# Scale steps of the float16 input projection: fixed places on VectorE, a unit more between them on TensorE, and the transpositions of queries and keys a unit later

## The chip, the cores and the metric

One NeuronCore of a Trainium2 chip runs the whole kernel. The metric is the device time of one execution in microseconds (us). Before the change it was 2442.49 us, the median of 3 runs (2439.93 to 2445.21). Five engines work side by side, each through its own instructions in order: TensorE (PE, matmuls and transpositions into PSUM), VectorE (DVE), ScalarE (ACT), GpSimd (POOL) and SyncE (SP, which here only issues DMAs). They wait for each other through semaphores.

## The reference

One layer of a hybrid decoder, on a sequence of 2048 rows with 1024 columns. Only the first half of it bears on the change:

```python
sh1, sc1, g1, sh2, sc2, g2 = jnp.split((c_act @ w_ada + b_ada)[:, None, :], N_MOD, axis=-1)
h = rmsnorm(x, norm1_g) * (1 + sc1) + sh1
proj = h @ w_in                       # 1024 x 3080
q, k, v, fg, xin, bg, cg = jnp.split(proj, IN_SPLITS, axis=-1)
q = rmsnorm(q.reshape(b, s, ATTN_HEADS, HEAD_DIM), q_norm_g)
k = rmsnorm(k.reshape(b, s, ATTN_HEADS, HEAD_DIM), k_norm_g)
attn = forgetting_attention(q, k, v, log_sigmoid(fg + b_forget))
conv = bg * causal_dwconv(cg * xin, conv_mix_w)
x = x + g1 * (jnp.concatenate([attn, conv], axis=-1) @ w_out)
# then a gated feed-forward network with a causal convolution (w_up, w_down)
```

## The kernel before, in words

**Numbers in two halves.** The projection runs in float16, and every operand is held as a high and a low half: hi = float16(scale x raw) and lo = scale x raw - hi. `scaled_split` makes them, the high half on ScalarE (L195), the low one on VectorE (L196). A product takes three matmuls (`mm3`, L142): hi hi, hi lo, lo hi. The scale is a power of two that comes from the data: `weight_group` sums the magnitudes of each raw weight tile on ScalarE (`weigh`, L191), takes the largest on VectorE (L215), and `power_of_two` brings it to all partitions in two steps. Its first step is a transposition on TensorE (L170), with a maximum and a small product on VectorE (L172, L173); its second a matmul with ones on TensorE (L176), and five tiny VectorE instructions (L177 to L181). Only then can the splits begin.

**Stages on TensorE.** From 0 to 54 us the modulation of the first normalization is computed, interleaved with the first of four chunks of h. Up to about 163 us the values are projected, 16 units of 128 rows: `transpose_in` turns a chunk of x, one column block k at a time (L348), ScalarE evacuates it with scale and shift (L350), GpSimd and VectorE make the two halves (L136, L353; chunk 0 in other forms first, L355 and L356). Chunk 0 of the values still uses unscaled weights; later ones use `wv16`, split by `first_scales`. ScalarE evacuates each value unit (L454, L455). Then come the key units (16, to 257.7 us), the query units (16, to 359.7), four conv groups of 64 us each (twelve units each, products for x, c and b of four chunks), and from about 627 us attention, the output projection and the feed-forward network.

**Key and query units (`project`).** A unit is 24 matmuls of 128x512. Behind it ScalarE squares the result (sq, L632), VectorE sums and takes the reciprocal root (r, rqt; L634 and L123 to L129) and scales (qn, L638). `finish` transposes qn on TensorE (L606), in the middle of a later unit: of the unit two behind. ScalarE evacuates the transposition (tf, L612), GpSimd and VectorE split it (th, tl; L136, L614) and SP stores the halves (L616). In between, hooks of single units do other work: `piece`, part of the later modulation, sums rows of `w_ada` that SP loads (L660) on VectorE into mo (L662, L664), and a piece later multiplies the sum on TensorE (L669 or L684); others make the cumulative sum of the forget gates (L525) and the largest value (L562).

**What sets the order.** Instructions given to K (`keep_in_program_order`) keep their place on their engine in program order; matmuls and transpositions all do. The others are placed by the scheduler. `weight_group` and `first_scales` are generators: each `next(group)` at the end of a unit carries out the part up to the next yield, so a yield is a distance of one unit. The magnitudes of `w_up` for the feed-forward network are also taken during these stages: `magnitudes` reduces one 128x512 tile on ScalarE (wx, L708) and has SP load the next into the only wx buffer (L713); both are pinned, twice in each of the units of a `lull` (key units 0 to 12, query units 2 to 14) and once behind each conv unit.

**Buffers.** PSUM tiles with the tag "tr" (transpositions, scale steps, L525, L562, the modulation products) share the two buffers of ps_t; unit results have six in ps_m. Raw weights (wr), high (wh) and low (wl) pairs have eight each, vt, qn and wm two, wx one.

## Time and profile before

| what | us |
|---|---|
| median of 3 runs | 2442.49 |
| the profiled execution | 2440.35 |
| its span on the core | 2438.5 |
| TensorE busy | 2336.2 (96%) |
| VectorE busy | 1802.1 (74%) |
| ScalarE busy | 1307.1 (54%) |
| GpSimd busy | 338.6 (14%) |

A row of a timeline gives the start and the duration in us, the engine, the line, the operation and its tiles (out<-in), and in brackets how long the engine was idle just before and which instruction of which engine ended the wait. A row of a window gives its length and the busy time and count of each engine in it, the granted clock of TensorE (1.00 is full), the busy share of the DMA engines and GB/s.

### The profile page before, as it was taken

To read this page: it belongs to the slowest core of one execution; us is meant where nothing else is said; L and a number is where in the kernel's file an instruction comes from. 1 tells how busy PE (TensorE), PEld (TensorE's weight loads), DVE (VectorE), ACT (ScalarE), POOL (GpSimd) and SP (SyncE) were. 2 spreads that over 40 slices of the span, in tenths; PEclk is the share of its full clock that TensorE was granted. 3 is DMA by queue.
4 is the path that set the end of the run, shared out by engine and by line. 5 is a ranking of instruction groups with operands and counts; after the bars stand their busy time and mean duration, and the time that the engine had idled before them with its cause. 6 is when DMAs were issued, how large, how long until landed. Compare 5 with 4: busy or idle time off the path is not lost.

```text
span 2438.5 us, 38643 instructions
## 1 busy us (share of the span) xinstructions
PE 2336.2 (96%) x14472; PEld 1405.9 (58%) x14472; DVE 1802.1 (74%) x3430; ACT 1307.1 (54%) x2136; POOL 338.6 (14%) x282
## 2 busy tenths in 40 slices
PE   5899989999899998999999999999999999999999
PEld 5764444444577776444444444788864444448887
DVE  6767785553799898456888888757768888985554
ACT  5644454321588897343665665554546556554333
POOL 0210101111577784001000000000000000000000
PEclk9999999999999999999999999999999999999999
DMA  9337687541599997534222222676742222236775
GB/s 278 126 105 193 156 244 208 157 127 44 109 182 187 227 183 144 179 108 151 82 92 87 87 87 86 201 247 217 229 134 87 87 87 88 92 103 210 229 227 183
DMA packets 428707, 368.71 MB, mean 151 GB/s; under 512 B 184208, under 2 KB 327912, under 8 KB 427496
## 3 DMA queue, kind: packets, MB, share of 16 engines
q1 hardware_dynamic: 421400, 349.40, 51.4%
q10 hardware_dynamic: 4752, 8.46, 1.0%
q0 software_dynamic: 2368, 8.39, 0.9%
q8 instruction: 113, 1.85, 0.3%
q14 instruction: 74, 0.61, 0.1%
HBM read 267.54 MB, written 65.08 MB: 136 GB/s over the span
## 4 chain that ended last, share of the span: by engine, by line
PE 72%; DVE 4%; ACT 2%; issue 2%; DMA 1%; POOL 0%; SPq 0%; ACTq 0%; DVEq 0%
PE acc L1360 33%; PE acc L142 24%; PE pr L142 6%; PE pt L1041 2%; PE ps L980 1%; PE ps L981 1%; DVE near L1048 1%; PE po L1077 1%; PE po L1079 1%; PE po L1078 1%; ACT s_t L1021 1%; DMA far<-wide 1%; DVE s_t L1004 1%; PE pt L1201 1%; DVE t L1177 0%
## 5 line engine op out<-in xcount | busy, mean ns | idle before, releaser
L1360 PEld LDWEIGHTS <-pair 128*128 128x128 f16 x3696 | 361.4, 98 | 436.3 <-issue 0.3
L1360 PE MATMUL acc<-t,pair 128*128 128x512 f16 x2112 | 477.4, 379 | 0.0
L1360 PE MATMUL acc<-b,pair 128*128 128x512 f16 x1584 | 363.5, 379 | 0.0
L1332 DVE TENSOR_TENSOR lo<-raw,hi 128x1024 fp32r<-128x1024 f32 x176 | 212.0, 1224 | 154.2 <-ACT hi L1331 153.9
L142 PE MATMUL acc<-hi 128*128 128x512 f32 x704 | 277.0, 394 | 1.6 <-DVE t L1177 1.5
L1331 ACT ACTIVATE hi<-raw 128x1024 fp32r<-128x1024 f32 x176 | 182.3, 1055 | 177.5 <-PE acc L142 142.4
L142 PE MATMUL acc<-lo,hi 128*128 128x512 f32 x704 | 274.5, 390 | 0.5 <-DVE lo L1332 0.5
L142 PE MATMUL acc<-hi,lo 128*128 128x512 f32 x704 | 274.4, 390 | 0.0
L1373 DVE SCALAR_TENSOR_TENSOR w<-w,fcw,w 128x1024 f32<-128x1024 f32 x176 | 226.1, 1285 | 34.6 <-ACT w L1368 25.2
L142 PEld LDWEIGHTS <-h 128*128 128x128 f16 x1344 | 130.6, 98 | 98.8 <-DVE h L353 4.6
L1184 ACT ACTIVATE pair<-raw 128x1024 f16<-128x1024 f32 x132 | 138.3, 1049 | 68.4 <-DVE raw L1267 68.4
L1368 ACT ACTIVATE w<-w,fcw 128x1024 f32<-128x1024 f32 x88 | 100.7, 1144 | 130.7 <-DVE w L1266 130.7
L142 PE MATMUL acc<-wp,mp 128*128 128x512 f16 x768 | 169.4, 379 | 1.1 <-DVE raw L933 1.0
L1021 ACT ACTIVATE s_t<-s_t,nb,cst 128x2048 f32<-128x2048 f32 (+15 forms) x128 | 164.7, 1288 | 5.1 <-ACT nb L1018 0.4
L1187 DVE TENSOR_TENSOR pair<-raw,pair 128x1024 f16<-128x1024 f32 x132 | 160.9, 1219 | 4.7 <-ACT pair L1184 4.7
L708 ACT ACTIVATE wx<-wx 128x512 f32<-128x512 f32 x88 | 55.4, 629 | 178.8 <-DMA wx<-in_w_up_dram 156.1
L142 PEld LDWEIGHTS acc<-hi 128*128 128x128 f32 x704 | 132.2, 188 | 31.4 <-DVE t L1177 4.4
L142 PEld LDWEIGHTS acc<-hi,lo 128*128 128x128 f32 x704 | 132.2, 188 | 27.8
L142 PEld LDWEIGHTS acc<-lo,hi 128*128 128x128 f32 x704 | 132.3, 188 | 27.5 <-DVE lo L1332 1.1
L1033 POOL TENSOR_TENSOR wide<-s_t,wide 128x1024 f16<-128x1024 f32 x64 | 136.7, 2136 | 5.3
L1004 DVE CUSTOM_DVE_ANT_0 s_t<-ps,nf,mx 128x512 f32<-128x512 f32 (+1 forms) x192 | 119.5, 644 | 16.6 <-PE ps L983 8.2
L142 PE MATMUL pr<-h,wl 128*128 128x512 f16 x576 | 127.0, 382 | 0.0
(344 smaller groups left out, 4212.3 us busy)
## 6 DMA issues: line engine op xcount, KB each, us to landing
raw<-in_w_up_dram SPq DMA_DIRECT2D x88, 512.0 KB, 3.7
raw<-y_sc SPq DMA_DIRECT2D x176, 256.0 KB, 4.1
raw<-in_w_down_dram SPq DMA_DIRECT2D x176, 256.0 KB, 5.9
wx<-in_w_up_dram SPq DMA_DIRECT2D x88, 256.0 KB, 2.8
y_sc<-w SPq DMA_DIRECT2D x44, 512.0 KB, 2.6
wm<-in_w_ada_dram SPq DMA_DIRECT2D x128, 128.0 KB, 2.7
wr<-in_w_in_dram SPq DMA_DIRECT2D x40, 256.0 KB, 4.2
x_t<-in_x_dram SPq DMA_DIRECT2D x16, 512.0 KB, 4.6
```

The source lines that it names most:

```text
L142: ins = T.matmul(acc, lhsT=a, rhs=b, start=st, stop=sp)
L708: K(A.activation(t, t, AF.Abs, accum_out=l1[:, n : n + 1]))
L1004: K(V.tensor_tensor_reduce(out=s_t[:, o0 + c0 : o0 + c0 + cw], in0=ps[:, 0:cw], in1=nf[:, c0 : c0 + cw], scale=1.0, scalar=-3.0e38 if g == ...
L1021: K(A.activation(cols, cols, AF.Exp, bias=nb[:, p : p + 1], scale=qk[:, 4:5], accum_out=un["l"][:, p : p + 1]))
L1033: K(G.tensor_tensor(wide[:, 1, :], s_t[:, WB * P : WU], wide[:, 0, :], op=ALU.subtract))
L1184: K(A.activation(hi, raw, AF.Copy))
L1187: K(V.tensor_tensor(lo, raw, hi, op=ALU.subtract))
L1331: K(A.activation(hi, raw, AF.Copy))
L1332: K(V.tensor_tensor(lo, raw, hi.bitcast(F32), op=ALU.subtract))
L1360: K(T.matmul(acc, lhsT=a, rhs=b, start=st, stop=sp, skip_group_check=True))
L1368: K(A.activation(y, u[:, 0:1024], AF.Copy, scale=fcw[:, ct : ct + 1]))
L1373: K(V.scalar_tensor_tensor(y, u[:, m : m + 1024], fcw[:, m * 44 + ct : m * 44 + ct + 1], y, op0=ALU.mult, op1=ALU.add))
```

## The change

Four things are done. The new file has its own line numbers; where two rows speak of the same line, the text gives both.

1. **Places on VectorE.** The instructions of `power_of_two`, `scaled_split` and `first_scales`, and the low half of the first value weights (a function of its own now, `rest_of_weight`), go to K and so keep their program order.
2. **Distances on TensorE.** `weight_group` yields once more between the transposition (L170) and the matmul with ones (L176), so this and all splits come a unit later; groups of conv columns from the second on make two splits a step instead of one.
3. **First scales.** Their transposition and ones product move into the early loop, ahead of and among the products of its last blocks; the eight splits of the value weights are made in two fours, the sums of squares of chunk 1 a step later.
4. **Queries and keys.** `finish` runs when three results wait instead of two (a unit later), with four qn buffers instead of two; the last three key units are finished in the first three query units, the last three query units in the first conv units. `running_offset` (L525) is hooked to key unit 4 instead of 5, and `next(first)` stands at block 0 of value unit 3 instead of block 2.

The core of the diff:

```diff
-            V.tensor_reduce(top[:, 0:1], pt[0:n, 0:P], axis=AX.X, op=ALU.max)
+            K(V.tensor_reduce(top[:, 0:1], pt[0:n, 0:P], axis=AX.X, op=ALU.max))
...
         def scaled_split(pair, raw, scale):
             hi, lo = pair
-            A.activation(hi, raw, AF.Copy, scale=scale)
-            V.scalar_tensor_tensor(lo, raw, scale, hi, op0=ALU.mult, op1=ALU.subtract)
+            K(A.activation(hi, raw, AF.Copy, scale=scale))
+            K(V.scalar_tensor_tensor(lo, raw, scale, hi, op0=ALU.mult, op1=ALU.subtract))
...
                 chain = power_of_two(ps_t, m, rw, top)
                 next(chain)
                 yield
+                yield
                 next(chain, None)
...
                     pairs.append([p.rearrange("p (k n) -> p k n", n=shape[-1]) if len(shape) == 3 else p for p in pair])
-                    yield
+                    if n % at_once == 0:
+                        yield
...
-                [P, 4, P], ("wh", "wl")[j % 2],
+                [P, 4, P], ("wh", "wl")[j % 2], 2 if j else 1,
...
                     scaled_split(pair, rv[k], hs[:, 1:2])
                     wv16.append(pair)
+                    if k == 3:
+                        yield
...
+            first = first_scales()
             for k in range(KD + 2):
                 if k < KD:
                     modulation(k, () if k else normalize(0))
                 if 0 < k <= KD:
+                    if k == KD:
+                        next(first)
                     rest()
                 if k < KD:
+                    rest_of_weight(k)
                     rest = transpose_in(0, k)
                 if k == KD - 1:
                     load_x(1)
                     load_x(2)
+                    next(first)
+                if k == KD:
                     norms = normalize(1)
                     next(norms)
                 if k >= 2:
                     for t in range(3):
                         value_products(early[t], 0, t, k - 2)
+                        if k == KD and t == 1:
+                            next(first)
...
-                            if (i, k) == (3, 2):
+                            if (i, k) == (3, 0):
                                 next(first)
...
-                    if k == MID and len(normed) == 2:
+                    if k == MID and len(normed) == 3:
                         finish(*normed.pop(0))
...
-                qn = bp.tile([P, H, DH], F32, tag="qn", name="qn")
+                qn = bp.tile([P, H, DH], F32, tag="qn", name="qn", bufs=4)
...
-{0: largest_gains, 1: gain_scales, 3: running_sum, 5: running_offset, 7: largest_value, 9: value_scale}, (0, 13), group)
+{0: largest_gains, 1: gain_scales, 3: running_sum, 4: running_offset, 7: largest_value, 9: value_scale}, (0, 13), group)
-{0: last_k, 1: last_k, 3: piece, 6: piece, 9: piece, 12: piece, 15: piece}, (2, 15), convs[0][2])
+{0: last_k, 1: last_k, 2: last_k, 3: piece, 6: piece, 9: piece, 12: piece, 15: piece}, (2, 15), convs[0][2])
...
-                        if (j, ch, k) == (0, 0, MID) and name in "xc":
+                        if (j, ch, k) == (0, 0, MID):
                             last_q()
```

**ScalarE, from the third value unit's evacuation to chunk 1.** vt<-pv is the evacuation of a value unit, hf that of a transposed block of x, wv_... the high half of a value weight. Before:

```order
L455 ACTIVATE vt<-pv 128x252
L458 DMA v_sc<-vt 128x512
L195 ACTIVATE wv_813<-wvr,scales 128x520
L195 ACTIVATE wv_816<-wvr,scales 128x520
L195 ACTIVATE wv_819<-wvr,scales 128x520
L195 ACTIVATE wv_822<-wvr,scales 128x520
L195 ACTIVATE wv_825<-wvr,scales 128x520
L195 ACTIVATE wv_828<-wvr,scales 128x520
L195 ACTIVATE wv_831<-wvr,scales 128x520
L195 ACTIVATE wv_834<-wvr,scales 128x520
L350 ACTIVATE hf_856<-pt,sh_135,a_134 128x512
```

And now, where L470 and L471 are the evacuations L454 and L455 of before, L474 is L458, and L355 is L350:

```order
L474 DMA v_sc<-vt 128x512
L191 ACTIVATE junk_w,group<-wr 128x512 x3
L470 ACTIVATE vt<-pv 128x260
L471 ACTIVATE vt<-pv 128x252
L474 DMA v_sc<-vt 128x512
L195 ACTIVATE wv_813<-wvr,scales 128x520
L195 ACTIVATE wv_816<-wvr,scales 128x520
L195 ACTIVATE wv_819<-wvr,scales 128x520
L195 ACTIVATE wv_822<-wvr,scales 128x520
L355 ACTIVATE hf_856<-pt,sh_135,a_134 128x512
```

Four splits instead of eight stand between the last evacuation of the first three units and that of the transposed block; the other four are ahead of the first evacuation, and magnitude passes of the key weights (L191) stand among the evacuations.

**TensorE, in the seventh query unit** (unit 22 of the two projections). pt<-ident,qn is a transposition of `finish`, pm a modulation product. Before:

```order
L142 LDWEIGHTS h_1_723
L142 MATMUL acc<-wl,h_1_723 128x512
L606 MATMUL pt<-ident,qn 128x128 x4
L669 MATMUL pm<-ones,mo 128x1 x2
L142 LDWEIGHTS h_1_709
L142 MATMUL acc<-wl,h_1_709 128x512
```

And now, where L622 is L606 of before and L685 is L669:

```order
L142 LDWEIGHTS h_1_746
L142 MATMUL acc<-wl,h_1_746 128x512
L622 MATMUL pt<-ident,qn 128x128 x4
L176 MATMUL pt<-group,ones 128x1
L685 MATMUL pm<-ones,mo 128x1 x2
L142 LDWEIGHTS h_1_732
L142 MATMUL acc<-wl,h_1_732 128x512
```

Three takers of the two ps_t buffers stand in a row where two stood; the ones product of the group (L176) came a unit earlier before. In the eighth key unit L176 has in the same way come between the transposition and the one of L562.

**VectorE, in the second conv group.** group is the scale of the next group's weights, mo the running modulation sum, z and y the tiles of the convolution, gates a result of the modulation. Before:

```order
L664 SCALAR_TENSOR_TENSOR mo<-wm,cact,mo 128x256 x6
L800 SCALAR_TENSOR_TENSOR z<-pr,group,z 128x512
L172 TENSOR_REDUCE group<-pt 1x1
L173 TENSOR_SCALAR group<-ident,group 1x1
L813 SCALAR_TENSOR_TENSOR y<-z,cst,y 128x512
L814 SCALAR_TENSOR_TENSOR y<-z,cst,y 128x512
L177 TENSOR_SCALAR group<-pt 128x1
L178 TENSOR_SCALAR group<-group 128x1
L179 RECIPROCAL group<-group 128x1
L685 TENSOR_TENSOR gates<-pm,gates 128x256
L180 TENSOR_SCALAR group<-group 128x1
```

And now (L680 is L664 of before, L816 is L800, L829 to L832 are L813 to L816, L701 is L685, L678 is L662):

```order
L680 SCALAR_TENSOR_TENSOR mo<-wm,cact,mo 128x256 x6
L816 SCALAR_TENSOR_TENSOR z<-pr,group,z 128x512
L172 TENSOR_REDUCE group<-pt 1x1
L173 TENSOR_SCALAR group<-ident,group 1x1
L829 SCALAR_TENSOR_TENSOR y<-z,cst,y 128x512
L830 SCALAR_TENSOR_TENSOR y<-z,cst,y 128x512
L701 TENSOR_TENSOR gates<-pm,gates 128x256
L831 TENSOR_TENSOR y<-y,bt 128x512
L678 TENSOR_SCALAR mo<-wm,cact 128x256
L832 TENSOR_REDUCE vmax<-y 128x1
L680 SCALAR_TENSOR_TENSOR mo<-wm,cact,mo 128x256 x3
L177 TENSOR_SCALAR group<-pt 128x1
```

The first step (L172, L173) keeps its place behind the six sums of mo and the product z; the second (L177), which waits for TensorE's L176, comes behind y's products and the first sums of the next piece.

53 lines of the change are left out of this document (28 added, 25 removed).

## The prediction

> **What bounds the kernel now.** I read the page's busy shares first, then TensorE's waits up to 660 us, then windows and timelines around each wait.
>
> ```profile
> span 2438.5 us, 38643 instructions
> PE 2336.2 (96%) x14472; PEld 1405.9 (58%) x14472; DVE 1802.1 (74%) x3430; ACT 1307.1 (54%) x2136; POOL 338.6 (14%) x282
> 626.00:2438.50 1812.50, 1766.95 (x11382) 1084.90 (x11381) 1408.55 (x2268) 1044.32 (x1566) 260.69 (x178) 1.00 0.53 148
> ```
>
> TensorE (PE) is the bound: 96% busy. The third row is a window (length, busy time of PE, weight loads, VectorE, ScalarE, GpSimd; then granted clock, DMA share, GB/s): from 626 us, where attention begins, nothing of the change is left, so those 1812.5 us stay. The change can only win back time in which TensorE waits, or runs at half clock, before that. TensorE's waits there (engine, line, what it waited for: us, times, longest):
>
> ```profile
> PE pt L348 <- ACT hf L350: 7.0, 5, 6.2
> PE pt L606 <- DVE qn L638: 5.8, 6, 1.9
> PE pt L176 <- DVE group L173: 5.4, 1, 5.4
> PE pt L606 <- DVE rqt L127: 2.5, 1, 2.5
> PE pv L142 <- DVE hl L356: 2.4, 1, 2.4
> PE po L525 <- DVE group L172: 2.3, 1, 2.3
> PE pt L606 <- ACT sq L632: 1.6, 1, 1.6
> ```
>
> These seven rows sum to 27.0 us. Some waits are followed by a lower granted clock, which costs again (the column behind the five busy times):
>
> ```profile
> 61.00:64.00 3.00, 2.99 (x18) 2.91 (x19) 0.00 (x0) 1.40 (x4) 0.00 (x0) 0.69 0.58 99
> 64.00:66.00 2.00, 2.00 (x12) 2.00 (x12) 1.56 (x10) 0.00 (x0) 0.00 (x0) 0.62 0.88 145
> 78.70:82.00 3.30, 3.30 (x16) 3.17 (x17) 2.79 (x5) 3.00 (x5) 1.81 (x3) 0.50 0.94 315
> 342.00:346.00 4.00, 4.00 (x12) 1.47 (x11) 3.73 (x16) 1.50 (x5) 0.00 (x0) 0.57 0.96 250
> 464.00:468.00 4.00, 4.00 (x11) 1.87 (x11) 2.99 (x10) 0.00 (x0) 1.00 (x2) 0.50 0.23 80
> ```
>
> Length times (1 - clock) is what each loses: 0.9 + 0.8 = 1.7 us behind the wait at 61 us, 1.6 behind that at 79, 1.7 behind that at 340, 2.0 behind that at 464. All together, 27.0 + 7.0 = 34 us, or 1.4%, is the most that is to be had.
>
> **The values (54 to 163 us).**
>
> ```profile
> 61.01 0.39 PE L142 MATMUL pv<-wh,hl 128*128 128x260 f32 x1 [2.41 <-DVE hl L356]
> 67.43 2.74 DVE L343 TENSOR_SCALAR x_t<-x_t,ss 128x1024 f32<-128x1024 f32 x4
> 72.89 5.06 ACT L195 ACTIVATE wv<-wvr,scales 128x520 f16<-128x520 f32 x8 [1.31 <-DVE scales L181]
> 77.85 1.42 ACT L350 ACTIVATE hf<-pt,sh,a 128x512 f32<-128x512 f32 x2
> 78.66 0.90 PE L348 MATMUL pt<-ident,x_t 128*128 128x128 f32 x3 [6.23 <-ACT hf L350]
> 82.00:92.00 10.00, 7.51 (x58) 5.50 (x57) 10.00 (x14) 8.99 (x16) 5.26 (x6) 0.97 0.49 166
> ```
>
> The last low half of chunk 0 (L356) is now issued ahead of the sums of squares, so the 2.41 us and the slow 1.7 us behind it go. But the next thing TensorE needs, the scaled x of chunk 1 (L343), still ends at about 67.43 + 2.74 = 70.2 us: the early gain runs into that wait, and I count it at nothing by 70 us. What is worth more is the 6.23 us at 78.66: the transposed chunk's evacuation (L350) stood behind eight splits of the value weights (L195, 5.06 us) that themselves waited for the spread-out scale steps. Now four splits stand ahead of the evacuation of the first value units and only four between, half of 5.06 us: 2.5 us come back, and up to 4 if the second four start with their scales long ready. ScalarE's four magnitude passes of w_k (L191) now stand in front of them; they wait for loads, which is why I don't take more. In 82 to 92 us TensorE is idle for 2.5 of 10 us among evacuations and splits of h that alternate on ScalarE; the evacuations now go first, the splits later: 0 to 2 us. The first four splits also stand ahead of an evacuation (L454) that frees a slot for the first unit: up to 2.5 us lost if no x is waited for. Sum: 4.5 us won, range 1 to 7.5. Small waits for h near 140 us may go too: 0.5, range 0 to 1.5.
>
> **Keys and queries (163 to 374 us).**
>
> ```profile
> 163.00:257.70 94.70, 91.44 (x454) 45.11 (x453) 74.23 (x299) 39.88 (x94) 9.02 (x16) 1.00 0.63 171
> 340.57 0.63 PE L606 MATMUL pt<-ident,qn 128*128 128x128 f32 x4 [1.85 <-DVE qn L638]
> 199.11 0.38 PE L525 MATMUL po<-cum,blk 128*128 128x1 f32 x2 [2.33 <-DVE group L172]
> 199.00:203.00 4.00, 3.89 (x19) 1.90 (x20) 2.99 (x14) 2.25 (x6) 0.62 (x1) 1.00 0.56 151
> 208.85 3.17 ACT L195 ACTIVATE wl<-wr,group 128x512 f16<-128x512 f32 x5 [1.02 <-DVE group L181]
> 232.32 0.63 ACT L708 ACTIVATE wx<-wx 128x512 f32<-128x512 f32 x1 [5.35 <-DMA wx<-in_w_up_dram]
> 264.69 0.63 ACT L708 ACTIVATE wx<-wx 128x512 f32<-128x512 f32 x1 [2.91 <-DMA wx<-in_w_up_dram]
> L708 ACT ACTIVATE wx<-wx 128x512 f32<-128x512 f32 x49 | 30.8, 629 | 83.1 <-DMA wx<-in_w_up_dram 82.9
> ```
>
> *Removed.* With a third unit between a projection and its transposition (one unit is 24 matmuls, 94.7 us / 16 = 5.9 us in this stage), the waits for qn, rqt and sq at L606 (5.8 + 2.5 + 1.6 = 9.9 us, the longest 2.5) have 5.9 us more room and go; so do the 2.3 us at L525, where the cumulative sum's product is moved off the spot that shared its PSUM buffers with the scale step, and the 1.7 us of low clock at 342. Together 13.9 us.
>
> *Added.* The transpositions, the scale products and the sums of the modulation share two PSUM buffers (ps_t). At two places three takers now stand in a row: L606, L176, L562 after the eighth key unit, and L606, L176, L669 after the seventh query unit. The third must wait until ScalarE has evacuated the transposition just made (L612). How long that takes is shown by transpositions of before at those places:
>
> ```profile
> 210.56 0.38 PE L606 MATMUL pt<-ident,qn 128*128 128x128 f32 x2
> 213.63 0.67 ACT L612 ACTIVATE tf<-pt,gq 128x512 f32<-128x512 f32 x1
> 299.73 0.38 PE L606 MATMUL pt<-ident,qn 128*128 128x128 f32 x2
> 303.33 2.54 ACT L195 ACTIVATE wh<-wr,group 128x512 f16<-128x512 f32 x4
> 307.19 0.67 ACT L612 ACTIVATE tf<-pt,gq 128x512 f32<-128x512 f32 x1
> ```
>
> 213.63 + 0.67 - 210.56 = 3.7 us, and 307.19 + 0.67 - 299.73 = 8.1 us. The second stood behind a run of group splits (303.33) that are now spread out, so I take 4 and 5.5, with bounds of 2 and 8.1 for the second, 2 and 5 for the first: 9.5 us, from 4 to 13. A wait as long as these may lower the clock as the others did: 0 to 3.4, taken at 1. Last, the splits of the query weights: they were made in a bunch (five of eight at 208.85); now one per unit, in ScalarE's order between the passes over w_up (L708), the last behind the 25th, which came at 264.69 in before. The first query unit wants the last pieces about 4 us after its start at 257.7. ScalarE reaches its 25th pass only as fast as the one wx buffer is reloaded (the last row of the group: 82.9 of 83.1 us idle are waits for it). So the wait is between 0 (chain 3 us earlier as the keys start earlier, and no bunch of raw loads, whose gap of 5.35 us at 232 goes) and 264.7 + 0.7 + 0.6 - 261.7 = 4.3 us, plus about 2.7 us, a load's gap, if the passes begin one load later: 0 to 7, taken at 2. Sum added: 12.5, from 4 to 23. Net: 1.4 won, from 10 won to 9 lost. The queues passed: SP's w_q and group loads now stand singly between the wx loads; the key stores move a unit later, and SP's reloads of them for attention with them, as far behind as before. The 4-deep qn ring costs space only.
>
> **Conv groups (360 to 626 us).**
>
> ```profile
> 360.00:424.00 64.00, 63.30 (x305) 30.05 (x306) 37.84 (x102) 26.72 (x63) 8.18 (x12) 1.00 0.76 212
> 457.76 1.00 DVE L664 SCALAR_TENSOR_TENSOR mo<-wm,cact,mo 128x256 f32<-128x256 f32 x2 [2.69 <-DMA wm<-in_w_ada_dram]
> 460.44 0.49 DVE L664 SCALAR_TENSOR_TENSOR mo<-wm,cact,mo 128x256 f32<-128x256 f32 x1 [1.69 <-DMA wm<-in_w_ada_dram]
> 462.01 0.48 DVE L664 SCALAR_TENSOR_TENSOR mo<-wm,cact,mo 128x256 f32<-128x256 f32 x1 [1.07 <-DMA wm<-in_w_ada_dram]
> 463.37 0.20 DVE L173 TENSOR_SCALAR group<-ident,group 1x1 f32<-1x1 f32 x1
> 463.72 0.55 PE L176 MATMUL pt<-group,ones 1*128 1x1 f32 x2 [5.39 <-DVE group L173]
> ```
>
> TensorE's scale product (L176) waits for VectorE's L173, which stands behind modulation sums that wait for their weights. L176 now stands a unit later, two behind the transposition it follows (L170) instead of one; twelve units make a group of 64 us (the first row), 5.3 us each, and the wait is 5.39. What stands at the old place now, the product of the modulation (L684), needs sums (mo) of the piece before, so nothing takes the wait over. 5.39 + 2.0 of low clock go: 7.4, range 5 (if up to 1 us of the wait and some low clock stay) to 7.4. If the cover is gone, because those weights come 5.3 us later still, it is 0. The splits, now two a step, end no later than one a step did.
>
> **Sum.** 4.5 + 0.5 + 1.4 + 7.4 = 13.8 us. The profiled execution took 2440.35 (its span 2438.5 and 1.85 around it): 2426.5. The median of the runs shown lies 2.1 higher: 2428.6. Bounds, all terms together: 1 + 0 - 9 + 5 = -3, and 7.5 + 1.5 + 10 + 7.4 = 26.4: 2445.5 to 2416.
>
> [...] The clock fell behind waits of 2.41 us (at 61) and 1.85 us (at 340.6), and not behind 2.33 us at 199, where the rows go on unslowed. [...]
>
> A wait for a PSUM buffer is the price of this change: L525 shows one of 2.33 us with three takers in a row. [...] The trace has the one gap only; the case in which it repeats is the second rival.
>
> **Rivals.**
>
> *All the waits go and no new one comes* (faster than forecast): ScalarE is less bunched, evacuates within 2 us, and the query weights are in time. For it: 5.9 us more room at each unit. Against: ScalarE lags by up to 8.1 us behind the transpositions and that lag is set by w_up's loads. It gives 2442.5 - 26.4 = 2416. Chance 0.17.
>
> *The wait for the two buffers repeats* (no change): not only L562 and the first L669 but the three later L669 of the query units wait too. These need the evacuation of the transposition one unit before, 5.9 us back; at the lag of 8.1 us each waits 2.2. Three are 6.6, and the first costs 8.1 instead of 5.5: 9.2 us more, 13.8 - 9.2 = 4.6 won, 2437.9. For it: ScalarE's lag grows with the wx loads, and a TensorE that waits less runs further ahead of it. Against: the 8.1 had the bunch of splits in it, the 3.7 didn't. Chance 0.18.
>
> *SP's queue lengthens the chain of wx passes* (slower): the raw loads for the conv groups, eight in this stage, now stand one by one between wx loads, and each waits in SP's order until a split of a query weight, made between two passes, frees its buffer; the wx load behind it waits too. One such round costs a wx gap, 2.9 us by the row at 264.69; eight are 23 us, less the 5.35 gone with the bunch, 18. 13.8 - 18 = -4, and with the values at their low end -8: 2446 to 2450. It decides from 13.8 + 4.9 = 19 us of such delay, 15 with the values at their low end. For it: one wx buffer, and an idle time that is all waits for it. Against: a split takes 0.6 us, and it stands ahead of the pass that frees the buffer for the wx load in question. Chance 0.10.
>
> *The steps are pinned but VectorE is late at the new places* (the change doesn't do what it says): then conv gains nothing, 2442.5 - 6.4 = 2436. It is inside the forecast's range, at its slow end.
>
> **Chances.** Forecast 0.55, faster rival 0.17, same 0.18, slower 0.10. A measurement of this kernel can tell 0.2%, 4.9 us, from no change. Faster by more: 0.55 + 0.17 = 0.72; same 0.18; slower 0.10. The range takes in the faster rival down to 2415 and the same case and part of the slower up to 2446.
>
> **What would show it.** Right: no wait of over 1 us at L176 in the conv groups and full clock there (most certain); no waits for qn at L606; the wait for hf at L350 near 75 us at 2 to 4 us; two waits of 4 to 6 us, at L562 and L669, for ScalarE's evacuation. Wrong: waits at L142 for w_q's low parts in the first query unit above 5 us, the wx passes' gaps above 2.9 us, a ring wait at each L669, or TensorE waiting over 3 us for L454 near 65 us.

## The result, and the profile after

The changed kernel takes 2459.31 us, the median of 6 runs (2453.19 to 2462.07), against 2442.39 (6 runs, 2438.99 to 2447.73) for the kernel before: 1.0065 times as long, with a 95% interval of 1.0048 to 1.0083. That is 16 us slower, where 14 us faster were forecast. The profiled execution took 2461.88 us.

The page of the changed kernel shows the same number of matmuls and the same work on VectorE and ScalarE, in a longer span:

```profile
span 2460.2 us, 38616 instructions
PE 2349.2 (95%) x14472; PEld 1418.1 (58%) x14472; DVE 1804.1 (73%) x3430; ACT 1306.5 (53%) x2136; POOL 335.7 (14%) x282
```

To see where the time went, the starts of the same matmul are compared in both traces (the n-th of line L142 in TensorE's order; the products are the same in all kernels here). A number that grows down a column is time lost in that stage.

| product of L142 | what it is | before, us | after, later by | free_first_weights | two_wx_alone | gains_together |
|---|---|---|---|---|---|---|
| 96 | two thirds of the early products | 54.6 | +11.5 | -0.6 | -0.7 | -0.4 |
| 256 | chunk 1 of the values | 94.5 | +5.7 | -5.1 | -0.7 | -4.4 |
| 352 | chunk 2 of the values | 107.8 | +11.8 | +0.7 | -0.7 | -4.5 |
| 768 | first key unit | 162.9 | +10.9 | -1.0 | -0.7 | -4.9 |
| 1152 | first query unit | 257.7 | +15.5 | +3.6 | -2.0 | -7.7 |
| 1680 | first conv group | 394.8 | +20.6 | +3.9 | -11.1 | -18.1 |
| 2016 | second conv group, behind L176 | 477.1 | +16.1 | +0.3 | -17.1 | -25.4 |
| 2600 | last conv unit | 606.8 | +16.0 | +0.2 | -17.1 | -25.5 |

Behind the conv groups the profile of after loses 5.6 us more, with the same instructions as before. The clock stands there at half for 13.7 us (868.9 to 872.3, 971.3 to 978.2 and 1118.1 to 1121.5) against 3.4 us in before (953.0 to 956.4), which is up to 5.1 us. The other profiles differ there by -2.0 to +4.5 us, and the medians of all runs are 17 us apart, not 22, so most of it belongs to the two executions that were profiled and not to the change.

**The early loop** (0 to 66 us) loses 11.5 us. VectorE of before, where a step is L304 and L306 (sums of the modulation), L325 (low half of a value weight) and L356 (low half of h):

```profile
40.84 0.69 DVE L356 TENSOR_TENSOR hl<-hf,hh 128x512 fp32r<-128x512 f32 x1 [1.31 <-ACT hh L355]
41.45 0.61 DVE L304 TENSOR_SCALAR acc<-wa,cact 128x256 f32<-128x256 f32 x2
41.98 2.46 DVE L306 SCALAR_TENSOR_TENSOR acc<-wa,cact,acc 128x256 f32<-128x256 f32 x6
44.35 0.70 DVE L325 TENSOR_TENSOR wl<-wvr,wh 128x520 fp32r<-128x520 f32 x1
44.96 0.69 DVE L356 TENSOR_TENSOR hl<-hf,hh 128x512 fp32r<-128x512 f32 x1
```

VectorE of after (L308 is the sums, L332 the low half of the weight, L361 that of h):

```profile
37.12 2.46 DVE L308 SCALAR_TENSOR_TENSOR acc<-wa,cact,acc 128x256 f32<-128x256 f32 x6
39.50 0.68 DVE L361 TENSOR_TENSOR hl<-hf,hh 128x512 fp32r<-128x512 f32 x1
41.57 0.70 DVE L332 TENSOR_TENSOR wl<-wvr,wh 128x520 fp32r<-128x520 f32 x1 [1.39 <-ACT wh L326]
47.16 0.70 DVE L332 TENSOR_TENSOR wl<-wvr,wh 128x520 fp32r<-128x520 f32 x1 [1.38 <-ACT wh L326]
```

ScalarE of after, in the step between (sh and a are the evacuated modulation, wh the high half of the weight):

```profile
40.51 0.26 ACT L320 ACTIVATE sh<-pmod,cst 128x1 f32<-128x1 f32 x1 [2.61 <-PE pmod L317]
40.67 0.34 ACT L321 ACTIVATE a<-pmod,bg,cst 128x1 f32<-128x1 f32 x1
40.91 0.64 ACT L326 ACTIVATE wh<-wvr 128x520 fp32r<-128x520 f32 x1
```

A step was 44.96 - 40.84 = 4.1 us, with VectorE idle only once in a while. Now it is 47.16 - 41.57 = 5.6. The rows close a ring: VectorE's sums end at 39.58, TensorE turns them (pmod), ScalarE evacuates them at 40.51, only then makes the high half of a weight (40.91), and VectorE's low half waits for that (41.57); the next sums stand behind it. TensorE waits for the sums, more often than before. The first two rows are its waits of before and after in this loop, the third is one of them:

```profile
PE pmod L315 <- DVE acc L306: 20.3, 4, 13.8
PE pmod L317 <- DVE acc L308: 25.4, 7, 11.5
44.92 1.13 PE L317 MATMUL pmod<-ones,acc 128*128 128x1 f32 x8 [1.78 <-DVE acc L308]
```

Behind the waits of 1.8 us at 44.92 and 56.09 the clock falls to 0.50, from 46.3 to 49.7 and from 56.6 to 66.8 us; the last two steps take 6.1 and 6.4 us instead of 5.6.

**The values** win and lose. The answer to the wait of 6.23 us at 78.66 is the first row here, 2.98 us; the next rows are a new wait, at chunk 2, with what stands ahead of it on ScalarE and VectorE:

```profile
87.09 0.98 PE L353 MATMUL pt<-ident,x_t 128*128 128x128 f32 x4 [2.98 <-ACT hf L355]
106.88 2.56 ACT L195 ACTIVATE h<-hf,scales 128x512 f16<-128x512 f32 x4
110.19 2.73 DVE L196 SCALAR_TENSOR_TENSOR h<-hf,scales,h 128x512 f16<-128x512 f32 x4
115.74 1.11 PE L353 MATMUL pt<-ident,x_t 128*128 128x128 f32 x4 [3.15 <-ACT hf L355]
```

From product 96 to 256 5.8 us are won, from 256 to 352 6.1 are lost: the splits of h that used to alternate with the evacuations of chunk 1 now hold up those of chunk 2. The loss that the prediction put at up to 2.5 us came too: TensorE waits 2.74 us at 75.69 for the evacuation of a value unit (L470, formerly L454).

**Keys and queries.** TensorE's waits of after in this stage; none for qn, rqt or sq at the transposition (L622, formerly L606) is left:

```profile
PE pm L685 <- ACT tf L628: 7.3, 2, 4.7
PE pt L578 <- ACT tf L628: 5.8, 1, 5.8
PE acc L142 <- ACT wl L195: 3.8, 1, 3.8
PE acc L142 <- DVE wl L196: 0.9, 1, 0.9
PE pt L176 <- ACT tf L628: 0.3, 1, 0.3
```

The wait of 5.8 us at L578 (formerly L562), with the evacuation it waits for and what ScalarE did in between:

```profile
218.04 0.60 PE L622 MATMUL pt<-ident,qn 128*128 128x128 f32 x4
225.05 0.37 PE L578 MATMUL pt<-ident,vm 128*1 128x128 f32 x1 [5.76 <-ACT tf L628]
223.21 0.63 ACT L724 ACTIVATE wx<-wx 128x512 f32<-128x512 f32 x1 [4.36 <-DMA wx<-in_w_up_dram]
224.32 0.68 ACT L628 ACTIVATE tf<-pt,gq 128x512 f32<-128x512 f32 x1
```

ScalarE stands idle for 4.36 us, waiting for a tile of w_up, and the evacuation that TensorE needs is queued behind that pass. The low clock that follows these waits (windows; the granted clock is the third number from the end):

```profile
212.00:240.00 28.00, 21.97 (x99) 10.61 (x98) 17.35 (x74) 8.70 (x20) 2.47 (x4) 0.88 0.60 174
283.00:292.00 9.00, 8.74 (x31) 4.06 (x31) 7.28 (x32) 2.51 (x6) 0.62 (x1) 0.69 0.47 117
322.00:330.00 8.00, 4.22 (x13) 2.10 (x14) 5.75 (x24) 3.82 (x8) 0.62 (x1) 0.57 0.77 198
```

Length times (1 - clock): 3.4 + 2.8 + 3.4 = 9.6 us (an upper bound, since the waits themselves lie in the windows). The clock is at 0.50 from 223.8 to 230.6, 281.8 to 288.7 and 322.8 to 329.6; behind the ends of the waits (225.05, 281.8 and 325.78) that leaves 16.3 us at half clock, so up to 8.1 us.

**Conv groups.** The wait at L176 has shrunk, not gone, and no low clock follows it any more:

```profile
486.11 0.48 DVE L680 SCALAR_TENSOR_TENSOR mo<-wm,cact,mo 128x256 f32<-128x256 f32 x1 [1.42 <-DMA wm<-in_w_ada_dram]
487.48 0.20 DVE L173 TENSOR_SCALAR group<-ident,group 1x1 f32<-1x1 f32 x1
487.74 0.38 PE L176 MATMUL pt<-group,ones 1*128 1x1 f32 x2 [2.77 <-DVE group L173]
487.70:492.00 4.30, 4.26 (x21) 2.13 (x22) 2.95 (x6) 0.06 (x1) 1.41 (x2) 1.00 0.26 86
```

### The profile page after: what moved, and what is told of

Its sections match the earlier page's. It is cut to its first block, busy times and chain, and to the rows that moved or that the text cites. A ratio compares the mean times of both kernels' runs of the same rounds, so it can differ in the third digit from the quotient of the medians.

```text
span 2460.2 us, 38616 instructions
## 1 busy us (share of the span) xinstructions
PE 2349.2 (95%) x14472; PEld 1418.1 (58%) x14472; DVE 1804.1 (73%) x3430; ACT 1306.5 (53%) x2136; POOL 335.7 (14%) x282
## 3 DMA queue, kind: packets, MB, share of 16 engines
q8 instruction: 113, 1.85, 0.3%
## 4 chain that ended last, share of the span: by engine, by line
PE 74%; DVE 7%; issue 7%; DMA 6%; ACT 5%; POOL 1%; SPq 0%; ACTq 0%; DVEq 0%; POOLq 0%
PE acc L1376 32%; PE acc L142 25%; PE pr L142 6%; DMA wx<-in_w_up_dram 3%; PE pt L1057 2%; PE pv L142 1%; PE ps L996 1%; PE ps L997 1%; DVE near L1064 1%; DVE s_t L1020 1%; PE po L1093 1%; PE po L1095 1%; PE po L1094 1%; DMA wm<-in_w_ada_dram 1%; ACT s_t L1037 1%
## 5 line engine op out<-in xcount | busy, mean ns | idle before, releaser
L142 PE MATMUL acc<-hi 128*128 128x512 f32 x704 | 277.1, 394 | 1.6 <-DVE t L1193 1.6
L142 PE MATMUL acc<-lo,hi 128*128 128x512 f32 x704 | 274.6, 390 | 0.5 <-DVE lo L1348 0.5
L142 PE MATMUL acc<-hi,lo 128*128 128x512 f32 x704 | 274.5, 390 | 0.0
L1389 DVE SCALAR_TENSOR_TENSOR w<-w,fcw,w 128x1024 f32<-128x1024 f32 x176 | 226.1, 1285 | 34.6 <-ACT w L1384 25.4
L142 PEld LDWEIGHTS <-h 128*128 128x128 f16 x1344 | 133.3, 100 | 104.1 <-issue 13.4
L142 PE MATMUL acc<-wp,mp 128*128 128x512 f16 x768 | 171.1, 382 | 1.1 <-DVE raw L949 1.0
L142 PEld LDWEIGHTS acc<-hi 128*128 128x128 f32 x704 | 132.3, 188 | 31.4 <-DVE t L1193 4.4
L142 PEld LDWEIGHTS acc<-hi,lo 128*128 128x128 f32 x704 | 132.3, 188 | 27.6
L142 PEld LDWEIGHTS acc<-lo,hi 128*128 128x128 f32 x704 | 132.4, 188 | 27.4 <-DVE lo L1348 1.1
L142 PE MATMUL pr<-h,wh 128*128 128x512 f16 x576 | 126.5, 380 | 0.0
```

What stands on the lines that cost most here:

```text
L142: ins = T.matmul(acc, lhsT=a, rhs=b, start=st, stop=sp)
L1389: K(V.scalar_tensor_tensor(y, u[:, m : m + 1024], fcw[:, m * 44 + ct : m * 44 + ct + 1], y, op0=ALU.mult, op1=ALU.add))
```

## The experiments

Times are medians; the ratio is to the kernel before, run beside it on the same chip, with its 95% interval. A difference of two ratios is turned into us with 2441. An interval reaches 2 to 5 us to each side, so such a difference is uncertain by 3 to 7 us; where it is smaller than that, only the traces can speak, each of one execution.

### The early loop

**free_first_weights**: the changed kernel with the first weights as in before.

```diff
-                K(A.activation(hi, raw, AF.Copy))
-                K(A.activation(junk_w[:, 0 : AW + H], raw, AF.Abs, accum_out=wsum[:, j : j + 1]))
+                A.activation(hi, raw, AF.Copy)
+                V.tensor_tensor(lo, raw, hi.bitcast(F32), op=ALU.subtract)
+                weigh(raw, AW + H, wsum[:, j : j + 1])
```

> The changed kernel with one part undone: the high half, the magnitudes and the low half of the eight unscaled value weights in the early loop are free for the scheduler again, as in before. Theory 1 (these three pins make a loop: VectorE's low half waits for ScalarE's high half, which stands behind the modulation's evacuation, which waits for TensorE and so for VectorE's sums; 5.6 to 6.3 us a step instead of 4.1): the 96th of L142's products comes near 55 us instead of 66, the first key unit starts at 163 to 165 instead of 173.9, the time falls by 9 to 12 us against the changed kernel, to about 6 us above before. Rival (the values are paced later, by the scaled x of chunk 1 and the splits, so an earlier start is waited away at 70 to 90 us): less than 4 us.

2443.8 us, 1.0023 [1.0002, 1.0044]: 10.3 us under the changed kernel by the ratios. One of the eleven runs, at 2471.1 us, pulls its ratio up; by the medians, 2.3 us above before here and 16.9 there, it is 14.6. Product 96 comes at 54.0, the first key unit at 162.0. Theory 1 holds. The early lead is kept: nothing later waits it away.

**pin_first_weights_alone**: the kernel before with that part alone.

```diff
+                K(A.activation(hi, raw, AF.Copy))
+                K(A.activation(junk_w[:, 0 : AW + H], raw, AF.Abs, accum_out=wsum[:, j : j + 1]))
+                wv.append((hi, lo, raw))
...
+                    rest_of_weight(k)
                     rest = transpose_in(0, k)
```

> The kernel before with only those three pins and the low half at its new place (rest_of_weight). Theory 1: 9 to 12 us slower than before, 2452; the sums of the modulation on VectorE come every 5.6 to 6.3 us. Rival (the loss needs the first scales in the early loop too, whose steps are pinned there): within 3 us of before.

2451.98 us, 1.0043 [1.0030, 1.0056], 10.5 us slower, with product 96 later by 11.4. The three pins alone do it.

**first_weights_pins_scalar** and **first_weights_pins_vector** share them out: ScalarE's two pins without VectorE's, and the other way round.

```diff
 # first_weights_pins_scalar, against pin_first_weights_alone
-                K(V.tensor_tensor(lo, raw, hi.bitcast(F32), op=ALU.subtract))
+                V.tensor_tensor(lo, raw, hi.bitcast(F32), op=ALU.subtract)
 # first_weights_pins_vector, against pin_first_weights_alone
-                K(A.activation(hi, raw, AF.Copy))
-                K(A.activation(junk_w[:, 0 : AW + H], raw, AF.Abs, accum_out=wsum[:, j : j + 1]))
+                A.activation(hi, raw, AF.Copy)
+                weigh(raw, AW + H, wsum[:, j : j + 1])
```

> The kernel before with only ScalarE's two pins of the first weights (high half and magnitudes); the low half on VectorE is free. In the order, VectorE's instructions stand as in the next kernel, and ScalarE has the high half and magnitudes behind the evacuations sh and a of the same step. Theory (the place on ScalarE, behind sh and a, makes the loop): 9 to 12 us slower than before, like all three pins together (2452). Rival (VectorE's place for the low half does): within 3 us of before.

> The kernel before with only VectorE's pin of the first weights: the low half ahead of the next step's sums (rest_of_weight); ScalarE's two instructions are free, and the scheduler has them ahead of sh and a of the same step. Theory (ScalarE's place makes the loop): within 3 us of before. Rival: 9 to 12 us slower.

2454.14 us, 1.0048 [1.0035, 1.0060], and 2439.3 us, 0.9992 [0.9982, 1.0001]. VectorE's order is the same in both, so it is not VectorE's pin. With ScalarE's pins, VectorE's low half waits as in the changed kernel:

```profile
42.03 0.63 ACT L324 ACTIVATE wh<-wvr 128x520 fp32r<-128x520 f32 x1
42.69 0.70 DVE L330 TENSOR_TENSOR wl<-wvr,wh 128x520 fp32r<-128x520 f32 x1 [2.15 <-ACT wh L324]
```

Without them the high half is made ahead of sh and a of its step, and the low half doesn't wait (first_weights_pins_vector):

```profile
38.68 0.62 ACT L324 ACTIVATE wh<-wvr 128x520 fp32r<-128x520 f32 x1
40.22 0.26 ACT L318 ACTIVATE sh<-pmod,cst 128x1 f32<-128x1 f32 x1 [0.30 <-PE pmod L315]
43.53 0.69 DVE L330 TENSOR_TENSOR wl<-wvr,wh 128x520 fp32r<-128x520 f32 x1
```

### The splits of h

**free_h_splits**: in the changed kernel, the splits of chunk 0 of h free for the scheduler.

```diff
-                            scaled_split((h_hi[k][0], h_lo[k][0]), hf0[k], rh)
+                            A.activation(h_hi[k][0], hf0[k], AF.Copy, scale=rh)
+                            V.scalar_tensor_tensor(h_lo[k][0], hf0[k], rh, h_hi[k][0], op0=ALU.mult, op1=ALU.subtract)
```

> The changed kernel with the eight splits of chunk 0 of h free for the scheduler (both halves), the rest pinned. Theory 2 (these splits cost some 6 us of ScalarE and VectorE wherever they stand; the pins moved that from 82 to 92 us to 107 to 116, where the chunk 2 transpositions wait): within 3 us of the changed kernel, the wait at 110 to 116 gone and one near 80 to 92 in its place. Rival (the place at 107 to 116 is the loss): 5 to 7 us faster than the changed kernel.

2455.43 us, 1.0050 [1.0038, 1.0063]: 3.7 us faster than the changed kernel, between the two, but not clear of noise. In the trace the wait at 115.7 is gone. From product 256 to 352 nothing is lost any more (6.1 us before this edit); but from 96 to 256 only 1.8 us are won instead of 5.8, for the splits stand among the first units' evacuations again. Of the 6.1 us about 4 only move, and some 2 were the place.

### Keys and queries

**takers_apart**: in the changed kernel, no three takers of ps_t in a row.

```diff
-7: largest_value, 9: value_scale}, (0, 13), group)
+8: largest_value, 10: value_scale}, (0, 13), group)
-3: piece, 6: piece, 9: piece, 12: piece, 15: piece}
+3: piece, 7: piece, 10: piece, 13: piece, 15: piece}
```

> The changed kernel with the largest value hooked to key unit 8 instead of 7 (value scale 10 instead of 9) and the modulation pieces of the query units to 3, 7, 10, 13, 15 instead of 3, 6, 9, 12, 15, so that no three takers of ps_t stand in a row. Theory 3 (the third taker waits for the evacuation of the transposition just made): the waits of 5.8 us (L562) and 4.7 us (L669) go, with the low clock behind them, and the time falls by 8 to 14 us against the changed kernel. Rival (ScalarE's chain of passes over w_up paces the stage, so the wait comes back at the next taker or at the query weights): less than 4 us, and the last query unit ends within 3 us of the changed kernel's 379.

2452.85 us, 1.0047 [1.0035, 1.0060]: 4.4 us faster than the changed kernel, not quite clear of noise. The 5.8 us at L578 are 0.8, those at L685 gone; but new waits for the evacuation stand at the next takers (2.3 at L622, 2.1 at L583), and at L176 of the second conv group TensorE, being earlier, waits 6.3 us instead of 2.8. Neither theory alone: the place counts, and part of what it wins is waited for later.

**two_splits_a_unit**: in the changed kernel, the default of `at_once` is 2.

```diff
-        def weight_group(srcs, shape, tag, at_once=1):
+        def weight_group(srcs, shape, tag, at_once=2):
```

> The changed kernel with two splits a unit for every weight group, not for the later conv groups alone. Theory 4 (the query weights come late since the eighth of their splits stands behind the 25th pass over w_up): the last now stands behind about the 16th, the waits of 3.8 and 0.9 us in the first query unit go with the low clock behind them, and 4 to 7 us of the time; the waits for ps_t at L562 and L669 stay at 4 to 6 us. Rival (the wait is for the chain of passes, not for the place of the splits): the first query unit still waits 3 us or more, or the time falls by less than 2 us.

2451.67 us, 1.0035 [1.0022, 1.0049]: 7.3 us faster than the changed kernel. The waits for the query weights are gone (so they were for the place of the splits; the first conv group sets its own number and keeps one a unit), but the next wait at L685 grows from 4.7 to 7.8 us.

**later_transpositions_alone**: the kernel before with part 4 of the change alone.

```diff
-                    if k == MID and len(normed) == 2:
+                    if k == MID and len(normed) == 3:
...
-                qn = bp.tile([P, H, DH], F32, tag="qn", name="qn")
+                qn = bp.tile([P, H, DH], F32, tag="qn", name="qn", bufs=4)
...
-5: running_offset, 7: largest_value
+4: running_offset, 7: largest_value
-{0: last_k, 1: last_k, 3: piece
+{0: last_k, 1: last_k, 2: last_k, 3: piece
```

> The kernel before with one part of the change: the transpositions of keys and queries a unit later, four qn buffers, the offset at key unit 4. No three takers of ps_t stand in a row in it. By the prediction's term: the waits for qn, rqt and sq at L606 and that at L525 (12.2 us, 13.9 with the low clock) go, and the time falls by 8 to 13 us. Rival (the chain of passes over w_up paces ScalarE, so TensorE waits for the evacuations, L612, instead): under 4 us, with new waits of L606 or L669 for ScalarE.

2440.89 us, 1.0001 [0.9993, 1.0010]: nothing. All the waits of 12.2 us that it was to remove are gone, and these stand in their place:

```profile
PE pm L669 <- ACT tf L612: 5.8, 3, 3.2
PE pt L176 <- DVE group L173: 1.5, 1, 1.5
PE pt L606 <- ACT tf L612: 1.4, 2, 0.9
PE pt L606 <- DVE group L172: 1.4, 1, 1.4
```

TensorE is 4.5 us ahead at the first query unit and 0.3 behind at product 1680. The passes over w_up explain it: the first 25 run from 168.8 to 264.7 us in before, from 167.7 to 263.8 here, from 181.4 to 279.8 in the changed kernel: 96, 96 and 98 us. They go on at their own pace, and ScalarE, which must make them in order, with them.

**two_wx_alone**: the kernel before, with two buffers for the tiles of w_up and each load issued a pass ahead. No part of the change is in it.

```diff
-            while up_tiles:
+            while len(up_tiles) > 1 or up_tiles and asked[0] == 88:
...
-            for n in range(seen[0], min(seen[0] + 1, 88)):
-                t = bp.tile([P, 512], F32, tag="wx", name="wx", bufs=1)
+            for n in range(asked[0], min(asked[0] + 2 - len(up_tiles), 88)):
+                t = bp.tile([P, 512], F32, tag="wx", name="wx", bufs=2)
```

> The kernel before with two buffers for the tiles of w_up (wx) and the load of each issued a pass earlier; the passes keep their places on ScalarE, one place later each. Theory (the chain of loads and passes paces ScalarE in the key and query units): the passes come as early as the units allow, and the waits for qn, rqt and sq at L606 (9.9 us) go without any change of distance; 6 to 12 us faster than before. Rival (the waits at L606 are of VectorE's or TensorE's own order): within 3 us of before, the waits stay.

2426.58 us, 0.9940 [0.9926, 0.9953]: 15 us faster than before, more than expected. The first 25 passes run from 168.1 to 243.7 us, 76 us instead of 96: one buffer had set their pace. The waits of TensorE from 54 to 400 us at L606 and L525 are down from 12.2 us to

```profile
PE pt L606 <- DVE qn L638: 1.3, 1, 1.3
PE pt L606 <- ACT tf L612: 0.8, 1, 0.8
PE po L525 <- ACT tf L612: 0.7, 1, 0.7
```

and ScalarE's wait for w_up, over more passes (160 to 370 us, 54 passes; before, 49 passes with 82.9 us), is

```profile
L708 ACT ACTIVATE wx<-wx 128x512 f32<-128x512 f32 x54 | 33.8, 627 | 29.5 <-DMA wx<-in_w_up_dram 23.2 <-DVE rqt L128 5.8
```

A wait of 2.2 us at L176 of the first conv group is new, while the 5.4 us of the second are gone: 6.0 of the 17.1 us at product 2016 are won there, which the expectation hadn't counted. In the key and query units the distance was not what was short.

**two_wx_later_transpositions** and **two_wx_changed**: the same edit in later_transpositions_alone and in the changed kernel.

> The later transpositions alone, with the two wx buffers. Theory: ScalarE no longer lags, the waits for the evacuations (L612) at L606 and L669 (7.2 us there) go too; within 2 us of the two wx buffers alone, since the distance then has nothing left to win. Rival (the two PSUM buffers cost by themselves): waits of L669 for L612 of 4 us or more stay, and it is slower than the two wx buffers alone by 3 us or more.

2429.46 us, 0.9953 [0.9940, 0.9966]: 3.2 us slower than the two buffers alone, by the ratios, which is inside their noise. The waits for the evacuation are down to 1.8 us, so ps_t costs little by itself. The new wait is 6.2 us at L176 in the first conv group, for VectorE's L173; in the traces, TensorE is 6.6 us behind two_wx_alone at product 2016. The rival's cause is refuted; its size (3 us slower), if it is real, came from another wait.

> The changed kernel with the two wx buffers. Theory: in the key and query units the waits for ScalarE at L562, L669 and for the query weights (18 us, and the low clock behind them) fall to under a third, 10 to 18 us faster than the changed kernel: 2441 to 2449. The early loop's loss of 11 us stays. Rival (ps_t's three takers in a row cost that by themselves): under 6 us faster.

2440.13 us, 0.9996 [0.9987, 1.0005]: 16.8 us faster than the changed kernel. The same five rows as above are now

```profile
PE pt L578 <- ACT tf L628: 2.7, 1, 2.7
PE pm L685 <- ACT tf L628: 1.5, 1, 1.5
PE acc L142 <- DVE wl L196: 0.7, 1, 0.7
```

The three takers stand in a row as before, the buffers are as many, and the waits fall from 18.1 to 4.9 us: one more SBUF buffer of another stream took away most of the waits at the PSUM buffers.

### The conv groups

**conv_distance_alone**: the kernel before with the extra yield and two splits a step for the conv groups from the second on.

```diff
                 next(chain)
                 yield
+                if conv:
+                    yield
                 next(chain, None)
...
-                    yield
+                    if not conv or n % 2 == 0:
+                        yield
```

> The kernel before with one part of the change: for the conv groups from the second on, the extra yield between the two scale steps and two splits a step. By the prediction's term: 5.0 to 7.4 us faster than before, the wait at L176 under 0.5 us and full clock behind it. Rival, after the changed kernel's 2.8 us at that place (the sums of the modulation hold VectorE's first step back further when TensorE doesn't wait for it): a wait of 2 us or more stays, and the gain is 3 to 5 us.

2435.39 us, 0.9976 [0.9967, 0.9985]: 5.9 us faster. The wait that stays at L176 is 1.38 us (not 1.75, as the next expectation has it), with the clock at 1.00 behind it.

**conv_distance_four_loads**: the same with `wm` in four buffers.

```diff
-                wm = bp.tile([P, 256], F32, tag="wm", name="wm")
+                wm = bp.tile([P, 256], F32, tag="wm", name="wm", bufs=4)
```

> The kernel before with the conv groups' distance and four buffers for the loads of the modulation's weights (wm) instead of two. Theory (the wait of 1.75 us that stayed at L176 is for sums that wait for loads issued one by one between those of w_up): the wait falls below 0.5 us, and the time by 1 to 3 us against the distance alone (2435.4). Rival (SP issues them no sooner, being held up by the one wx buffer): the wait stays above 1 us and the time within 1.5 us.

2430.59 us, 0.9958 [0.9944, 0.9972]: 4.4 us faster than the distance alone, hardly more than the noise. No wait at L176 is left in the conv groups. VectorE's first step comes when the sums have their loads; that, and not TensorE's lead alone, sets the end of the wait.

### Together

**three_causes_mended**: the changed kernel with the edits of free_first_weights, takers_apart and two_splits_a_unit.

> The changed kernel with the first weights free for the scheduler, the takers of ps_t apart and two splits a unit everywhere. If the three causes are all there is: 9 to 12 (first weights) + 6.5 (takers, as measured) + 4 to 7 (query weights) under the changed kernel's 2459.3, so 2434 to 2440, 2 to 7 us faster than before. Rival (they overlap, since what one wins in the key and query units is waited for at the next step of ScalarE's chain): 2441 to 2446.

2438.74 us, 0.9986 [0.9977, 0.9995]: inside the first range, at its slow end. TensorE is 1.3 us ahead of before at product 1920, and the wait at L176 (5.9 us) comes at 468.55, 5 us after that of before: the gain of the conv groups is lost to the modulation's loads.

**early_scales_and_conv**: the kernel before with the early first scales (their steps and splits in the places of the change, the first weights and the splits of h free) and the conv distance; **and_later_keys**: that, with the keys' transpositions a unit later (and four qn buffers, the offset at key unit 4); **early_scales_four_loads**: the first, with wm in four buffers.

```diff
 # early_scales_and_conv: of part 3, as in the diff of the change
+            first = first_scales()
             for k in range(KD + 2):
...
 # and_later_keys, further
-                    if k == MID and len(normed) == 2:
+                    if k == MID and len(normed) == behind:      # 3 for keys, 2 for queries
```

> The kernel before with two parts of the change: the first scales in the early loop, with their splits in two fours, pinned, and the conv groups' distance. The first weights, the splits of chunk 0 of h, the scale steps on VectorE and all of the key and query units are as before. From the parts measured: the splits of h free again leave the values 5 us ahead at the first key unit, the conv groups win 6: 9 to 12 us faster than before, 2430 to 2433. Rival (the values' part is won by the pins of the scale steps alone, or the lead is lost in the key and query units): within 2 us of the conv distance alone, 2434 to 2437.

2434.67 us, 0.9966 [0.9953, 0.9978]. 4.2 us ahead at the first key unit and 4.5 at product 1920, and then L176 waits 4.4 us: by the time, nearer to the rival, but the lead is lost in the second conv group and not in the key and query units.

> The kernel above, with the transpositions of the keys alone a unit later (queries as before, two units behind), four qn buffers, the offset at key unit 4. The later transpositions alone were 4.2 us ahead in the key units and lost it in the query units, where the third unit's evacuations and the modulation products meet in ps_t. If the queries gave it back: 3 to 5 us faster than the kernel above. Rival (ScalarE's chain takes the lead back wherever it is won): within 2 us of the kernel above.

2437.81 us, 0.9982 [0.9973, 0.9991], slower than without: the rival. The lead of 8.9 us at product 1200 is 3.1 at product 1320, taken back by waits of 2.4 us for qn, 1.7 for the evacuation (L626) and 0.6 for a scale step, and by half clock from 270.1 to 273.5 us.

> The kernel with early first scales and the conv distance, and four buffers for the loads of the modulation's weights. Theory (the lead of 4 to 5 us from the values was taken back at L176 in the second conv group, where VectorE's sums wait for those loads): no wait over 1 us at L176, 3 to 5 us faster than without them (2434.7) and than the distance with four loads (2430.6): 2426 to 2430. Rival (the lead is taken back elsewhere): 2430 to 2435.

2425.69 us, 0.9937 [0.9923, 0.9950]: faster than both, and 7 us faster than without the four loads; no wait at L176, as the theory has it.

**gains_together**: early_scales_four_loads with the two wx buffers.

> The kernel with early first scales, conv distance and four loads (0.9937 of before), and the two wx buffers (0.9940 alone). If they are different times: key and query units win 11 us, the values 4, the conv groups under 6 (two wx buffers alone had won most of that wait already): 2412 to 2418. Rival (the second buffer had already won what the four loads win): 2419 to 2425.

2413.8 us, 0.9890 [0.9873, 0.9906]: the gains are different times for the most part, 27 us together by the ratio where the two alone were 15 and 15. It has pieces of three of the four parts of the change (the places of the first scales and their pins, the conv distance), without what the rest cost.

## Why the prediction was wrong

**The step that failed first: the part by part began at 54 us.** The change's first part says that the low half of the first weights goes to a function of its own with a fixed place, and the diff pins the high half and the magnitudes with it. The prediction gave these three pins no term: it took the pinning as a matter of VectorE's order and looked at ScalarE only from 61 us on. The row of 20.3 us at L315, the largest of TensorE's waits up to 660 us, stood outside its seven rows and its 34 us, as if nothing of the change could make it grow. The runs put 10 to 15 us on exactly these pins, and on ScalarE's two. A pin on an instruction that waits for nothing (the high half needs only its load) gave it the waits of what stands ahead of it.

**The values: a term of 4.5 us that was right by half.** The waits at 61 and 79 us shrank, 5.8 us by product 256 (4.5 in free_first_weights, where the early loop isn't late). The prediction let the splits of h go "later: 0 to 2 us" and named no work for them to stand behind or ahead of; they cost 6.1 us at chunk 2. That a part of this comes back when they are free is seen in one trace and is not clear in the time.

**Keys and queries: removed as forecast, added too small.** Every wait that was to go went. For the two third takers 9.5 us were forecast; they measured 5.8 + 4.7, and a third wait of 2.6 us came at a later L685. The query weights measured 4.7 where 2 was taken, within the range. The low clock was taken at 1 us, with 3.4 as its end; behind the waits it is up to 8.1. Together 9.7 us were lost from product 768 to 1680, a little over the slow end of the range (9 lost), where 1.4 won was taken. The second rival had the mechanism (ScalarE's lag grows with the loads of w_up, and a TensorE that waits less runs further ahead of it) and a chance of 0.18. two_wx_alone shows that it was the main thing: the waits at L606 were the end of a chain whose pace one buffer sets, and a longer distance only let TensorE meet it at the next place. It was named as "for it" of a rival and should have been the first question: who sets the pace of the engine that is waited for?

**SP's queue, the slower rival, did not come.** The first 25 passes took 98 us instead of 96, not 18 more. One of the signs of being wrong is no sign: gaps above 2.9 us between the passes came (4.36 us at 223.21), but before had them too (5.35 us at 232.32). That the time rose instead of falling has the causes above.

**Conv groups: right mechanism, 4.5 of 7.4 us** in the changed kernel (product 1680 to 2016), 5.9 in conv_distance_alone. Its own range began at 5, and the sign called most certain, no wait of over 1 us at L176, failed with 2.77. The prediction counted the cover at 5.3 us against a wait of 5.39, left open up to 1 us, and named as the other case only that the loads come a whole unit later. But the loads of the sums, which SP issues between those of w_up, set the end of the wait anew in each kernel: it was 1.4, 2.8 and 5.9 us in conv_distance_alone, the changed kernel and three_causes_mended.

**Sum.** Early loop 11.5, values 5.0 - 0.6 = 4.4 short, keys and queries 1.4 + 9.7 = 11.1 short, conv 7.4 - 4.5 = 2.9 short: 29.9 of the 30.7 us between 2459.3 and 2428.6.

## What to carry to other kernels

A fixed place makes an instruction inherit every wait ahead of it on its engine (here the two pins on ScalarE alone made it 1.0048 of before, the one on VectorE 0.9992): before pinning, list what each pinned instruction really needs and what it will now stand behind, on each engine that gets one, and not only on the one that the change names. More distance between a producer and its consumer wins nothing where a third stream sets the producer's pace (later_transpositions_alone: 1.0001 of before); look in the trace for what the late engine itself waits for (here 83 us of ScalarE's idle time on one load buffer) and double that first (two_wx_alone: 0.9940). A lead is only worth what the next wait whose end it doesn't move leaves of it (in early_scales_and_conv TensorE was 4.5 us ahead at product 1920, and the next wait at L176 was 4.4), so read the stage behind as well.

## What the runs showed of the hardware

The low clock was dearer than the 1 us that the prediction took, and the traces show when it came. Three pairs of windows of the changed kernel follow, each 3.41 us long and followed by the next one (busy time of TensorE is the second time, the clock the third number from the end):

```profile
83.87:87.28 3.41, 0.43 (x5) 0.23 (x4) 3.04 (x5) 3.41 (x6) 0.16 (x1) 1.00 0.46 139
87.28:90.69 3.41, 3.41 (x18) 3.15 (x18) 1.90 (x4) 2.35 (x5) 1.75 (x3) 0.50 0.69 245
111.17:114.58 3.41, 1.41 (x13) 1.05 (x11) 2.60 (x4) 1.79 (x4) 1.20 (x2) 1.00 0.00 0
114.59:118.00 3.41, 2.26 (x11) 1.88 (x12) 1.90 (x4) 2.95 (x5) 1.77 (x2) 0.50 0.01 2
483.23:486.64 3.41, 1.74 (x9) 0.59 (x6) 1.01 (x3) 0.87 (x3) 0.00 (x0) 1.00 0.54 158
486.64:490.05 3.41, 2.31 (x12) 1.24 (x13) 2.01 (x5) 0.43 (x1) 1.69 (x2) 1.00 0.40 115
```

TensorE is idle for 3.0 us in the first window and for 2.0 in the third, and half clock follows. In the fifth it is idle for 1.7, with the wait of 2.77 us at 487.7 divided between two windows, and full clock follows.

In the profiles of before and after the clock, recorded from 38.22 and 39.49 us on, is 1.00 or 0.50. But for the last of each, which ends with the program, a stretch at 0.50 lasts 3.41 us, 6.83 or, from 56.56 to 66.80 in after, 10.24. Divided into windows of 3.41 us at these changes, the two profiles have 1,387 with full clock. The 13 in which TensorE was idle for 2.0 us or more were all followed by half clock; of the 1,366 with less than 1.6 us idle none was, and of the 8 between 5 were. The waits at 340.6 and 199 us in the prediction lie in such cases between: TensorE of before is idle for 1.85 us from 338.59 to 342.01, with half clock behind it, and for 1.87 from 195.24 to 198.65, with full clock behind it. These are counts of two executions; what sets the clock they don't show.

By length times (1 - clock) 3.41 us at half clock cost up to 1.7 us. Behind four waits of after near 3 us (2.74 at 75.69, 2.98 at 87.09, 3.15 at 115.74 and 2.77 at 487.74) the clock was at 0.50 for 3.4, 3.4, 5.7 and 0 us, which is up to 1.6 us on average; so, as an estimate from these four, such a wait is better priced with about 1.5 us of low clock than without.
